# Keeping the last expert's block of the first layer on chip, and spreading the last combining products of the second

## The chip, the cores and the metric

The program runs on one core of one Trainium2 chip. The metric is the device time of one launch in microseconds (us): the median of three runs of the kernel before is 1739.39 us, with 1738.43 and 1743.01 us as the lowest and the highest. One more launch was recorded by the hardware profiler. All rows of a profile in this document come from that launch, and its times are counted from the start of its span.

The engines are named as the profile names them: PE (TensorE, matrix products; PEld is its weight load), DVE (VectorE), ACT (ScalarE), POOL (GpSimd) and SP (SyncE, which here only issues transfers). A name with a q, such as ACTq or SPq, is the engine's sequencer, which issues transfers and waits for semaphores.

## The reference

Two layers work on 512 tokens of `x` and 256 tokens of `ctx`, with 1024 features each, all in fp32.

```
for i in range(2):
    mod, modc = silu(c) @ mod_w[i] + mod_b[i], silu(c_ctx) @ mod_w[i] + mod_b[i]   # 6 parts each
    hx, hc = modulate(rmsnorm(x, ln1_g[i])), modulate(rmsnorm(ctx, ln1_g[i]))
    yx, yc = mixer_ab(hx, hc) if i == 0 else mixer_cd(hx, hc)
    x = x + g1 * yx
    hx = modulate(rmsnorm(x, ln2_g[i]))
    if i == 1:
        x = x + g2 * moe(hx)                       # 512 tokens
    else:
        ctx = ctx + g1c * yc
        out = moe(concat(modulate(rmsnorm(ctx)), hx))   # 768 tokens
        ctx = ctx + g2c * out[:256];  x = x + g2 * out[256:]
```

`moe` picks one of four groups and in it two of eight experts for each token. Each of the 32 experts computes `(silu(x @ w_gate) * (x @ w_up)) @ w_down` on its own tokens (1024 to 512 to 1024 features). The result, times the token's weight, is added to the token's row. `mixer_cd` of the second layer needs, for each token, the finished sum over its experts of the first layer: it starts with an RMS norm over the whole row, a modulation by a scale and a shift for each feature, and a product with `w_in_cd`, whose columns are the queries (512), the keys and values (256) and the pooled branch `u` (512).

## The kernel before

**Experts.** The experts are visited in an order of 32 steps, n = 0 to 31. Each step gathers up to 64 tokens (a second block of 64 is computed only where an expert has more than 64), and runs gate and up products (`mm_gate_up`, L1488, eight steps of k with one 512 KB page of weights each), `hidden`, `hidden_T` and the down products (`mm_down`, L1511, four pages). A block of 64 tokens fills 128 partitions: partitions 0 to 63 hold the first 512 features of the result and partitions 64 to 127 the last 512. The weights come through SP as pages of 512 KB in the order in which they are used.

**The end of a step in layer 0** (`main0`, L1556). `down(n)` multiplies the result by the token's weight and `g2` into a tile `ys` (`times_gate`, L1385: one ACT and two DVE instructions), and `scatter(n, 0)` adds its rows into the array `xD` in HBM with an indirect transfer of POOL (L1394). A second block has the same instructions for `ys`, and its store stands in a branch that POOL takes only for a count above 64. After step 31 come `next_weights(1, 2)`, which issues the first two pages of the query weights on ACT's queue, and `mixer_cd_in`.

**The start of the next mixer** (`mixer_cd_in`, L1813). Token tiles of 128 rows are handled in the order `seq = [0, 1, 4, 5, 2, 3]`; tiles 4 and 5 are `ctx` and have no queries and no `u`. `x_load` reads a tile X from `xD` on SP. `wkv`, `wq` and `wu` are weights that are split into a high and a low part: a step is one ACT instruction (`high`, L292) and one DVE instruction (`low`, L297) for each page, and frees the page. `rows(t)` makes the sum of squares on ACT (L271) and, when its second half `normed` is called, the factor (DVE L264, POOL L266) and the scaled rows `y` (DVE L1833). `trans(t)` transposes `y` on PE (L1848), applies scale and shift (six ACT instructions L1861 and two DVE instructions L1859) and splits the result into `hi` and `lo` (DVE L1863, L1864). In the loop over tiles, turn i projects tile i (`qkv`: 48 products, 24 for a `ctx` tile), then runs `rows` for tile i+2 and `trans` for tile i+1, the transposes of tile i-1's queries and keys, the 24 products `pu` of the branch `u`, and `qk_norm` and `qk_rotate`, whose last DVE instruction is L385. In turn 0 the four pages of `wu` are split between `qkv` and `rows`.

**Order and buffers.** In these stages every engine executes its instructions in the order in which the program writes them (`by_hand(4)` and `by_hand(5)`; only stages 3 and 6 leave some engines to the planner, L43). `sm` (L93) hands out four PSUM banks in turn, so a fifth small product waits until one of the last four has been read. `pages` (L99) hands out 4 KB pages of each partition, the longest free first; a transfer or an instruction that writes a page waits for the last reader of what it held before.

**Layer 1** (`main1`, L1598). The results of two steps are kept on chip as `hi` and `lo`, and are added to the token tiles by products with a one-hot matrix: `combine` (L1435) makes eight units, one for each half c of the features and each token tile t, of two products and one addition. For t = 1 of the very last pair the addition goes over ACT and POOL. During the gate and up products of the next odd step, `beside` (L1606) runs two units after each of k = 5, 6 and 7, and the rest after the last k. After step 31 the eight units of the last pair run at once, each followed by a store of 256 KB to the output on SP (L1620).

Of the kernel before, what the change touches and what calls it, by code (L numbers as in the profile page):

```python
# [7 lines left out]
F32 = mybir.dt.float32  # L8
# [62 lines left out]
def hybrid_dit_kernel(ctx: ExitStack, tc: tile.TileContext, a, out):  # L71
# [1250 lines left out]
    class Experts:  # L1322
# [112 lines left out]
        def combine(self, m, oh, then=None):  # L1435

            def unit(c, t):
                ps = sm("cmb")
                for i, y in enumerate(self.hl[m]):
                    nc.tensor.matmul(ps, oh[:, tok(t)], y[:, c * 512:(c + 1) * 512], start=(i == 0), stop=(i == 1))  # L1440
                if then and t % 3 == 1:
                    x, y = X(t)[:, c * 512:(c + 1) * 512], self.wp.tile([128, D], F32, tag="ys", name="ys", bufs=1)[:, 0:512]
                    nc.scalar.activation(y, ps, AF.Copy)
                    nc.gpsimd.tensor_tensor(x, x, y, OP.add)  # L1444
                else:
                    self.add(t, c, ps)
                if then:
                    then(t, c)

            return [lambda c=c, t=t: unit(c, t) for c in range(2) for t in range(self.nt)]  # L1450

        def block(self, b, w, tk):

# [102 lines left out]
        def main0(self):  # L1556
# [3 lines left out]
            NP = NE // 2  # L1560

            def down(n):
                t, e = hT[n], order[n]
                self.mm_down(self.yy[:, 0, :], 0, t, W[n, 2])
                when(cnti[0:1, e:e + 1], [PE], lambda: self.mm_down(self.yy[:, 1, :], 1, t, W[n, 2]))
                self.used((n, 2))
                self.scatter(n, 0)()
                when(cnti[0:1, e:e + 1], [POOL], self.scatter(n, 1))

# [28 lines left out]
        def main1(self):  # L1598
# [6 lines left out]

            def beside(n, k):  # L1606
                self.used_page((n, k // 4), k % 4)
                for _ in range(2 if k >= 5 else 0):
                    if units:
                        units.pop(0)()  # L1610

# [201 lines left out]
    def mixer_cd_in(m1, mk, work, QS, KS, v, us):  # L1813
# [11 lines left out]

        def rows(t):

            y = Y[t] = [pages.new("y", pools=[keep, m1] if t in seq[:2] else None) for _ in range(2)]
            ss = square_sum(mk, X(t), y[1])

# [61 lines left out]

        x_load(seq[0])
        run(wkv.steps)
        run(wq.steps)
        rest = load(a["w_in_cd"][1, 2:4], 2, [keep], nc.scalar)
        wq.raw.extend(rest)
        wq.step(rest[0])
# [3 lines left out]
            x_load(t)  # L1902
        wu = Split(load(a["w_in_cd"][2]), 512)
        router(1)
        rows(seq[0])()
        trans(seq[0])
        rows(seq[1])()
        for i, t in enumerate(seq):
            P[t] = big("qps")
# [149 lines left out]
        runs.append(run)  # L2059
        return run  # L2060

    runs, first = [], []

    def next_weights(i, n):
        first.append(load(a["w_in_cd"][i], n, [keep], nc.scalar))
# [147 lines left out]
```

## Time and profile before

| | |
|---|---|
| median of the runs | 1739.39 us (1738.43 to 1743.01) |
| the profiled launch's own time | 1740.23 us |
| its span, first to last instruction | 1738.6 us |
| PE busy | 1555.6 us, 89% of the span |
| DVE, ACT, POOL busy | 871.4, 498.0, 430.3 us |
| TensorE clock granted, mean | 0.965 of full speed |
| DMA, mean over the span | 306 GB/s read and written |

Busy time is summed over the launch; which engine or transfer a stage waits for has to be read from that stage. In the rows of a timeline, the columns are the start (us), the duration (us), the engine, the line of the kernel, the operation, the tile written and the tiles read, the shape and the number of instructions merged into the row; the brackets hold the time that the engine stood idle before it and what ended the wait. Where several instructions are merged, the duration is that of the whole group.

### The profile page before, as it was taken

To read this page: it belongs to the slowest core of one execution; us is meant where nothing else is said; L and a number is where in the kernel's file an instruction comes from. 1 tells how busy PE (TensorE), PEld (TensorE's weight loads), DVE (VectorE), ACT (ScalarE), POOL (GpSimd) and SP (SyncE) were. 2 spreads that over 40 slices of the span, in tenths; PEclk is the share of its full clock that TensorE was granted. 3 is DMA by queue.
4 is the path that set the end of the run, shared out by engine and by line. 5 is a ranking of instruction groups with operands and counts; after the bars stand their busy time and mean duration, and the time that the engine had idled before them with its cause. 6 is when DMAs were issued, how large, how long until landed. Compare 5 with 4: busy or idle time off the path is not lost. (4 is left out here: it accounts for less than half of the span.)

```text
span 1738.6 us, 23632 instructions
## 1 busy us (share of the span) xinstructions
PE 1555.6 (89%) x8524; PEld 823.2 (47%) x8524; DVE 871.4 (50%) x1674; ACT 498.0 (29%) x998; POOL 430.3 (25%) x376
## 2 busy tenths in 40 slices
PE   5979689998799999999987589989699999999996
PEld 4868457887333333333322477668433343232332
DVE  3797889788333332233232565775533443343334
ACT  3422458833111111111111443482211211111111
POOL 2535555132122122112111222310112212121110
PEclk9999889999799999999999899999799999999998
DMA  9211833356899999999999524623899999999996
GB/s 369 64 65 69 314 135 147 110 197 238 333 392 398 400 385 383 397 388 389 397 394 397 218 74 181 239 89 131 319 410 409 408 409 408 408 408 408 408 410 235
DMA packets 151567, 518.65 MB, mean 298 GB/s; under 512 B 22444, under 2 KB 23180, under 8 KB 151436
## 3 DMA queue, kind: packets, MB, share of 16 engines
q1 hardware_dynamic: 136748, 488.58, 71.8%
q0 software_dynamic: 11520, 16.81, 3.7%
q10 hardware_dynamic: 3168, 11.54, 1.7%
q8 instruction: 79, 1.29, 0.3%
q14 instruction: 52, 0.43, 0.1%
HBM read 510.49 MB, written 21.02 MB: 306 GB/s over the span
## 5 line engine op out<-in xcount | busy, mean ns | idle before, releaser
L1492 PE MATMUL gu<-w,xt 128*64 128x512 f32 x2304 | 535.4, 602 | 23.4 <-DMA w<-in_ex_dram 19.1
L1492 PEld LDWEIGHTS gu<-w,xt 128*64 128x64 f32 x2304 | 151.2, 137 | 348.1 <-issue 240.8
L1514 PE MATMUL yy<-w,ht 128*64 128x512 f32 x1152 | 272.5, 608 | 15.4 <-DMA w<-in_ex_dram 6.6
L1499 DVE TENSOR_TENSOR hh<-hh,gu 128x512 f32<-128x512 f32 (+1 forms) x64 | 35.4, 553 | 356.2 <-ACT hh L1498 356.2
L1498 ACT ACTIVATE hh<-gu 128x512 f32<-128x512 f32 (+1 forms) x64 | 31.4, 490 | 612.5 <-PE gu L1492 336.9
L1514 PEld LDWEIGHTS yy<-w,ht 128*64 128x64 f32 x1152 | 78.1, 138 | 183.5 <-issue 133.3
L1394 POOL DMA_INDIRECT xD<-ys,sidx x40 | 71.1, 1777 | 317.0 <-DVE ys L1390 314.5
L1405 DVE TENSOR_TENSOR X<-X,cmb 128x512 f32<-128x512 f32 x126 | 79.6, 683 | 99.9 <-PE cmb L1440 99.8
L1424 POOL TENSOR_TENSOR lo<-ys,hi 64x512 fp32r<-64x512 f32 x58 | 72.5, 1268 | 217.0 <-ACT hi L1423 217.0
L1367 POOL DMA_INDIRECT Xg<-hD,gidx x40 | 41.9, 1048 | 263.2 <-PE xtp L1476 243.6
L751 DVE SCALAR_TENSOR_TENSOR acc<-glu,convp,acc 128x784 f32<-128x784 f32 x76 | 97.9, 1288 | 1.6
L762 POOL TENSOR_TENSOR part<-part,prod 128x784 f32<-128x784 f32 x40 | 84.7, 2118 | 43.2 <-ACT prod L761 42.3
L1390 DVE TENSOR_TENSOR ys<-yy,ys 128x512 f32<-128x512 f32 x64 | 44.3, 692 | 96.9 <-PEq L1305 52.8
L266 POOL TENSOR_TENSOR rs<-ms,mhalf 128x1 f32<-128x1 f32 (+2 forms) x40 | 41.4, 1036 | 170.8 <-DVE ms L264 170.2
L1423 ACT ACTIVATE hi<-ys 64x512 fp32r<-64x512 f32 x64 | 40.2, 629 | 139.7 <-DVE ys L1401 139.7
L524 PE MATMUL ptp<-cst,P 128*128 128x128 f32 x368 | 52.9, 283 | 18.6 <-POOL P L512 10.5
L1508 DVE COPY ht<-htp 128x512 f32<-128x512 f32 (+1 forms) x64 | 35.4, 553 | 66.6 <-PE htp L1506 66.6
L697 PE MATMUL qps<-wh,hi 128*128 128x256 f32 (+1 forms) x176 | 61.0, 347 | 8.0 <-DVE hi L1863 2.4
L532 ACT ACTIVATE pT<-ptp 128x512 f32<-128x512 f32 (+1 forms) x96 | 53.3, 589 | 44.8 <-PE ptp L524 44.1
L512 POOL TENSOR_SCALAR P<-P,rd 128x768 f32<-128x768 f32 (+3 forms) x40 | 33.2, 829 | 130.9 <-DVE rd L510 41.9
L502 ACT ACTIVATE P<-S,nm 128x768 f32<-128x768 f32 (+3 forms) x80 | 59.9, 757 | 13.1 <-DVE nm L495 8.3
L495 DVE TENSOR_REDUCE nm<-S 128x1 f32<-128x768 f32 (+3 forms) x80 | 58.6, 763 | 8.2 <-PE S L488 5.9
(310 smaller groups left out, 2551.2 us busy)
## 6 DMA issues: line engine op xcount, KB each, us to landing
w<-in_ex_dram SPq DMA_DIRECT2D x768, 512.0 KB
w<-in_mod_w_dram SPq DMA_DIRECT2D x96, 512.0 KB
w<-in_w_out_dram SPq DMA_DIRECT2D x16, 512.0 KB
w<-in_w_in_ab_dram SPq DMA_DIRECT2D x14, 512.0 KB
hD<-x ACTq DMA_DIRECT2D x8, 512.0 KB
xD<-X ACTq DMA_DIRECT2D x6, 512.0 KB
w<-in_w_in_cd_dram ACTq DMA_DIRECT2D x6, 512.0 KB
X<-xD SPq DMA_DIRECT2D x6, 512.0 KB
```

The costliest lines, as they stand in the source:

```text
L495: nc.vector.tensor_reduce(nm, u["S"][h][:, u["span"]], AX.X, OP.max, negate=True)
L502: nc.scalar.activation(u["P"][h][:, :n], u["S"][h][:, u["span"]], AF.Exp, bias=nm, accum_out=u["den"][:, h:h + 1])
L524: nc.tensor.transpose(ps[:, (c - c0) * 128:(c - c0 + 1) * 128], u["P"][c // nk][:, c % nk * 128:(c % nk + 1) * 128], ident)
L532: nc.scalar.activation(dst, src, AF.Copy)
L697: nc.tensor.matmul(ps[:, o:o + n], h(x, k, tk), w(p, k, 0, n), start=(k == 0 and c == 0), stop=(k == KT - 1 and c == 2))
L751: nc.vector.scalar_tensor_tensor(acc, glu[:, ct, i:i + CW], w(i), acc, OP.mult, OP.add)
L762: nc.gpsimd.tensor_tensor(self.part[ct], self.part[ct], t, OP.add)
L1394: return nc.gpsimd.indirect_dma_start(out=xD[:, :], out_offset=bass.IndirectOffsetOnAxis(ap=idx, axis=0), in_=ys[:, :], in_offset=None, bo ...
L1405: nc.vector.tensor_tensor(x, x, ps, OP.add)
L1424: eng.tensor_tensor(lo[rows, c], ys[rows, c], hi[rows, c].bitcast(F32), OP.subtract)
L1492: nc.tensor.matmul(self.gu[c * 64:(c + 1) * 64, b, :], xt[:, k, q * 64:(q + 1) * 64], w[k][:, c * 512:(c + 1) * 512], start=(k == 0), stop ...
L1514: nc.tensor.matmul(yy[c * 64:(c + 1) * 64], t[:, b, f % 2, f // 2, :], w[f][:, c * 512:(c + 1) * 512], start=(f == 0), stop=(f == 3))
```

## The change

There are three edits.

1. In layer 0, the first block of expert step 31 is not scattered to HBM. Its rows `ys` are split into `hl` (a high part by an ACT copy and a low part by a DVE subtraction), and a one-hot matrix `oh` (768 columns, one for each token) is made from a POOL iota and a DVE comparison. Each `rows(t)` of the next mixer then multiplies `oh` and `hl` on PE (four products of 64 rows with 512 columns, two for each half of the features) and adds the two results to the loaded tile X on DVE, ahead of the sum of squares. The conditional store of a second block stays. `oh` and `hl` hold two pages until the last tile.
2. In `mixer_cd_in`, `rows` of the first tile comes between the splits of `wkv` and of the first two pages of `wq`; `normed` and `trans` of that tile come ahead of the load of the other two pages of `wq` (`rest`), of their splits, of the loads of the other five tiles and of the load of `wu`.
3. In layer 1, step 31 runs one combining unit after each k in place of two after each of the last three; and the eight units of a pair take the token tiles in the order 1, 0, 2, 3 in place of 0, 1, 2, 3.

```diff
@@ combine @@
-            return [lambda c=c, t=t: unit(c, t) for c in range(2) for t in range(self.nt)]
+            return [lambda c=c, t=t: unit(c, t) for c in range(2) for t in sorted(range(self.nt), key=lambda t: t % 3 != 1)]
@@ main0, down(n) @@
-                t, e = hT[n], order[n]
+                t, e, r = hT[n], order[n], self.route
+                if n == NE - 1:
+
+                    oh = pages.new("oh", F32R, (128, self.ntok), [keep])
+                    it, hl = pages.new("iotai", I32, (128, self.ntok)), pages.new("hl", F32R, (128, 2, 512), [keep])
+                    nc.gpsimd.iota(it, pattern=[[1, self.ntok]], base=0, channel_multiplier=0)
+                    nc.vector.tensor_scalar(oh, it, r.tok[:, 0, e:e + 1], None, op0=OP.is_equal)
+                    pages.done([it])
...
+                if n == NE - 1:
+                    ys = self.times_gate(0, r.ws[:, 0, e:e + 1], r.wc[:, 0, e:e + 1])
+                    nc.scalar.activation(hl[:, 0, :], ys, AF.Copy)
+                    nc.vector.tensor_tensor(hl[:, 1, :], ys, hl[:, 0, :].bitcast(F32), OP.subtract)
+                    when(cnti[0:1, e:e + 1], [POOL], self.scatter(n, 1))
+                    kept.extend((oh, hl))
+                    return
                 self.scatter(n, 0)()
@@ main1, beside(n, k) @@
-                for _ in range(2 if k >= 5 else 0):
+                for _ in range(1 if n == NE - 1 else 2 if k >= 5 else 0):
@@ mixer_cd_in, rows(t) @@
+            oh, hl = kept
+            for c in range(2):
+                part, ps = slice(c * 64, (c + 1) * 64), sm("cmb")
+                for i in range(2):
+                    nc.tensor.matmul(ps, oh[part, tok(t)], hl[part, i, :], start=(i == 0), stop=(i == 1))
+                x = X(t)[:, c * 512:(c + 1) * 512]
+                nc.vector.tensor_tensor(x, x, ps, OP.add)
+            if t == seq[-1]:
+                pages.done(kept)
@@ mixer_cd_in @@
         x_load(seq[0])
         run(wkv.steps)
+        normed = rows(seq[0])
         run(wq.steps)
+        normed()
+        trans(seq[0])
         rest = load(a["w_in_cd"][1, 2:4], 2, [keep], nc.scalar)
...
         wu = Split(load(a["w_in_cd"][2]), 512)
         router(1)
-        rows(seq[0])()
-        trans(seq[0])
         rows(seq[1])()
```

## Rows read from the trace of the kernel before

**Rows 1.** The windows view of four stretches from the end of layer 0's experts to the start of the next attention. The columns are the stretch, its length, the busy time and number of instructions of PE, PEld, DVE, ACT and POOL, the granted TensorE clock, the DMA share and GB/s.

```profile
968.00:982.00 14.00, 0.05 (x1) 0.08 (x2) 11.05 (x14) 4.67 (x6) 9.75 (x10) 0.68 0.69 227
...
996.10:1010.90 14.80, 14.80 (x82) 12.75 (x81) 8.95 (x16) 5.42 (x13) 4.03 (x3) 1.00 0.00 1
1010.90:1037.40 26.50, 20.35 (x135) 17.90 (x132) 17.60 (x37) 14.86 (x38) 6.83 (x8) 0.94 0.24 80
1037.40:1072.00 34.60, 34.60 (x190) 29.14 (x194) 18.51 (x35) 8.19 (x19) 9.21 (x8) 0.95 0.25 83
```

**Rows 2.** The timeline of PE over the same stretch: the first transposes of the mixer, the first projection, the first product `pu`, and the first product of the projections of tiles 1 and 2.

```profile
981.95 1.94 PE L1848 MATMUL tp<-cst,y 128*128 128x128 f32 x8 [14.14 <-DVE y L1833]
985.33 0.55 PE L697 MATMUL qps<-wh,hi 128*128 128x256 f32 x1 [1.44 <-ACT y L1861]
...
996.92 0.47 PE L697 MATMUL pu<-wh,hi 128*128 128x512 f32 x1
...
1002.48 0.39 PE L697 MATMUL qps<-wh,hi 128*128 128x512 f32 x1
...
1037.40 0.50 PE L697 MATMUL qps<-wh,hi 128*128 128x512 f32 x1 [2.41 <-DVE hi L1863]
```

**Rows 3.** The timelines of DVE, POOL, SP and ACT between layer 0's last down products and those transposes: the last expert's result, its scatter, the loads of the six tiles, the first sum of squares and the scaled rows.

```profile
967.95 0.69 DVE L1390 TENSOR_TENSOR ys<-yy,ys 128x512 f32<-128x512 f32 x1 [3.19 <-PEq L1305]
...
968.91 1.81 POOL L1394 DMA_INDIRECT xD<-ys,sidx  x1 [14.74 <-DVE ys L1390]
...
975.42 2.73 SPq L1824 DMA_DIRECT2D X<-xD  x6
...
979.03 1.06 ACT L271 ACTIVATE y<-X 128x1024 f32<-128x1024 f32 x1 [3.85 <-DMA X<-xD]
...
981.05 0.75 DVE L1833 TENSOR_SCALAR y<-X,rs 128x1024 f32<-128x1024 f32 x1 [0.69 <-POOL rs L266]
```

**Rows 4.** The timelines of ACT and DVE over the splitting of `wkv` and `wq`: two issues of `wq` pages, the two steps of `wkv`, the two issues of `rest` and the step on its second page, and DVE's six steps in one row.

```profile
963.13 0.86 ACTq L132 DMA_DIRECT2D w<-in_w_in_cd_dram  x2
964.17 2.00 ACT L292 ACTIVATE wh<-w 128x1024 fp32r<-128x1024 f32 x2 [0.55 <-DMA w<-in_ex_dram]
...
968.71 0.82 ACTq L132 DMA_DIRECT2D w<-in_w_in_cd_dram  x2
...
974.12 1.06 ACT L292 ACTIVATE wh<-w 128x1024 fp32r<-128x1024 f32 x1 [0.82 <-DMA w<-in_w_in_cd_dram]
...
970.42 7.76 DVE L297 TENSOR_TENSOR wl<-w,wh 128x1024 fp32r<-128x1024 f32 x6
```

**Rows 5.** The timelines of ACT, SP and DVE around the first transposes: the six modulations of tile 0, the issue of the four pages of `wu`, ACT's first and last step on them, DVE's four steps on them, and the first modulation on DVE of tile 1.

```profile
983.12 2.20 ACT L1861 ACTIVATE y<-tp,modT,A 128x128 f32<-128x128 f32 x6 [2.94 <-issue]
...
987.79 1.06 ACT L292 ACTIVATE wh<-w 128x1024 fp32r<-128x1024 f32 x1 [1.43 <-DMA w<-in_w_in_cd_dram]
...
991.63 1.06 ACT L292 ACTIVATE wh<-w 128x1024 fp32r<-128x1024 f32 x1 [0.16 <-DMA w<-in_w_in_cd_dram]
...
978.24 2.67 SPq L132 DMA_DIRECT2D w<-in_w_in_cd_dram  x4
...
988.88 5.18 DVE L297 TENSOR_TENSOR wl<-w,wh 128x1024 fp32r<-128x1024 f32 x4
...
998.02 0.41 DVE L1859 TENSOR_SCALAR y<-tp,A,modT 128x128 f32<-128x128 f32 x1 [2.49 <-ACT y L1861]
```

**Rows 6.** The timeline of DVE in turns 1 to 3 of the loop over tiles: three times the last instruction of a turn's `qk_rotate` and the next tile's first modulation.

```profile
1009.69 0.42 DVE L385 TENSOR_TENSOR ks<-qn,ks 128x256 fp32r<-128x256 f32 x1
...
1012.69 0.41 DVE L1859 TENSOR_SCALAR y<-tp,A,modT 128x128 f32<-128x128 f32 x1 [0.21 <-ACT y L1861]
...
1025.04 0.42 DVE L385 TENSOR_TENSOR ks<-qn,ks 128x256 fp32r<-128x256 f32 x1
...
1027.73 0.41 DVE L1859 TENSOR_SCALAR y<-tp,A,modT 128x128 f32<-128x128 f32 x1
...
1033.95 0.43 DVE L385 TENSOR_TENSOR ks<-qn,ks 128x256 fp32r<-128x256 f32 x1 [1.02 <-ACT ks L382]
...
1036.48 0.41 DVE L1859 TENSOR_SCALAR y<-tp,A,modT 128x128 f32<-128x128 f32 x1
```

**Rows 7.** Two groups of the lines view over the whole span: the addition of a PSUM bank to a tile, and the high part of `ys` in layer 1. The columns are the line, the engine, the operation, tiles and shapes, the count, the busy time in us and the mean of one in ns, the idle time before and what ended it.

```profile
L1405 DVE TENSOR_TENSOR X<-X,cmb 128x512 f32<-128x512 f32 x126 | 79.6, 683 | 99.9 <-PE cmb L1440 99.8
...
...
L1423 ACT ACTIVATE hi<-ys 64x512 fp32r<-64x512 f32 x64 | 40.2, 629 | 139.7 <-DVE ys L1401 139.7
```

**Rows 8.** The timelines of PE and DVE in the last step of layer 1: the gate and up products of k = 0 to 4, of k = 6 and of k = 7, the first product of the units between them and of those after k = 7, and DVE's last four additions.

```profile
1705.61 4.46 PE L1492 MATMUL gu<-w,xt 128*64 128x512 f32 x20
...
1712.39 1.08 PE L1492 MATMUL gu<-w,xt 128*64 128x512 f32 x4
1713.40 0.50 PE L1440 MATMUL cmb<-hi,oh 128*128 128x512 f32 x1
...
1714.53 1.08 PE L1492 MATMUL gu<-w,xt 128*64 128x512 f32 x4
...
1716.31 2.48 DVE L1405 TENSOR_TENSOR X<-X,cmb 128x512 f32<-128x512 f32 x4 [0.85 <-PE cmb L1440]
```

**Rows 9.** The timelines of POOL and SP at the end of the span: the first addition of POOL to a tile, and the eight stores of the output, of which the first starts at the time shown and the other seven follow that addition.

```profile
1729.86 1.29 POOL L1444 TENSOR_TENSOR X<-X,ys 128x512 f32<-128x512 f32 x1 [39.30 <-ACT ys L1443]
...
1729.61 5.35 SPq L1620 DMA_DIRECT2D out_dram<-X  x8
```

More of the change, by code (lines that the diff above doesn't have):

```diff
@@ L2060, in extra_slot @@
         return run
-    runs, first = [], []
+    runs, first, kept = [], [], []
     def next_weights(i, n):
```

## The prediction

> **What bounds the kernel now.** I read the busy shares first: PE is busy for most of the span, so a change is worth what it does to stretches in which PE waits. The windows view shows where these are. Between 968 and 982 us PE does next to nothing; up to 1010.9 and again from 1037.4 to 1072 us it is busy throughout; between 1010.9 and 1037.4 it idles 6.2 of 26.5 us [rows 1]. PE's timeline gives the waits: 14.14 us for the scaled rows of the first tile, and 2.41 us for DVE's `hi` of tile 2 at 1037.40 [rows 2]. The other engines' timelines say what lies in the 14.14 us. The last result is ready at 968.64, its scatter starts at 968.91, SP issues the tile loads at 975.42, ACT squares at 979.03, DVE writes `y` at 981.05 [rows 3]. The wait covers other work: ACT and DVE split `wkv` and `wq` in it, DVE until 978.2 [rows 4], and SP issues `wu` in it [rows 5]. In the loop over tiles the chain passes DVE, ACT and POOL in turn: from a turn's last L385 to the next tile's L1859 there are only 2.1 to 2.6 us [rows 6].
>
> The sum is made against the profiled launch, 1740.23 us; its span is 1738.6, so 1.63 us lie around it. The median is 0.84 us below it. All engines here keep program order, so I walk the new order with the old durations.
>
> **Edit 1 and 2, up to the first transposes.** The scatter of step 31 and the wait for it go. The tile load then waits for the scatter of step 30, long past, and is free. What is late next is the sum itself. `ys` ends at 967.95 + 0.69 = 968.64. ACT's copy takes 0.63, as L1423 does [rows 7]; the subtraction takes 0.69, as the multiplication of the same size did [rows 3]: `hl` is ready at 970.05. The scatter's second `ys`, scale and rope stand next in DVE's queue and took from 968.64 to 970.42 [rows 3, 4], 1.78: DVE is free at 971.85. ACT waited for `ys` too: behind its copy are queued the second block's copy, the issue of the first `wq` pages (at 963.13 before), and the splits of `wkv` (at 964.17 before) [rows 4], now at about 970 to 972. The two `low` steps of `wkv`, 7.76 / 6 = 1.29 each [rows 4], end at 974.5. The four products have run by then. I bound one, which has 64 rows where before shows none so shaped in this stage, by nothing and by 0.6, and both are covered by the `low` steps. Two additions, 2.48 / 4 = 0.62 each [rows 8], 0.68 by the group [rows 7], end at 975.8. The square holds ACT until 977.0. Then come the two `high` steps of `wq` (2.0), whose `low` steps end at 980.75, and only behind them, in DVE's queue, the factor and `y` (0.75). From the square's start to the start of `y` there were 2.02 us, of them 1.06 for the square itself [rows 3], so the factor, with POOL, takes 0.9: `y` ends at 982.4. PE starts at 982.5 in place of 981.95. The expected gain of several us is a loss of 0.5; I take 0.5 and keep 0 to 1; a gain is excluded as long as DVE keeps its order.
>
> **Edit 2, after the first transposes.** `rest` was issued at 968.71 and used at 974.12 for its second page [rows 4], inside the wait. Now its issue stands behind six instructions L1861, which ended at 985.32 [rows 5]: 985.8. Of the five other tile loads, the last takes the page of tile 0's `y` (walking the list of free pages), which the transposes free at about 984.5, and `wu`, issued at 978.24 before [rows 5], stands behind it on SP. So seven pages are asked for between 984.7 and 987.2. Pages land (991.63 - 987.79) / 3 = 1.28 us apart [rows 5], and the second page of `rest` took 5.41 us [rows 4], so 2.85 ahead of the first. Alone it would land at 991.2; as the last of the seven at 984.7 + 2.85 + 7 x 1.28 = 996.5. In order of issue it is the fifth: 994.0, which I take.
>
> From there one queue follows another. ACT splits that page until 995.1, DVE until 996.4. Only then come tile 1's additions (997.7), its square on ACT, and 2.05 after the square's start (979.03 to 981.05 [rows 3]) its `y`, until 1000.5. ACT's steps on `wu` stand behind that square, so that DVE's four steps, 5.18 [rows 5], run from 1000.5 to 1005.7; before, they ran from 988.88 beside the first projection. Behind them are the additions of the third tile (1007.0), its square, factor and `y` (1009.8), and behind these tile 1's first L1859: 1009.8 in place of 998.02 [rows 5], 11.8 late. PE can't fill this: the products of the third tile's rows and the transposes of tile 1 hold all four small banks, so `pu` waits for the first of those additions (1006.4 in place of 996.92 [rows 2]). With the landing at 991.2 the delay is 9.0, at 996.5 it is 14.3.
>
> **The loop.** From the end of L385 to the next L1859 there were 2.58, 2.27 and 2.10 us [rows 6], 6.95 in all, because the square could run during the projection. Now the products of `rows` stand behind the projection on PE and the additions behind L385 on DVE: 1.3 + 2.05 + 0.75 + 0.1 = 4.2 us a tile, 12.6 in all: 5.65 more. It ends with tile 2's projection (1037.40), after which no tile has `rows` left, and PE is busy without a gap to 1072 [rows 1], so nothing takes the delay back. The extra products on PE, at most 24 at some 0.3 us, lie in the waits. The iota and the comparison for `oh` lie beside the down products, where POOL waits 14.74 us and DVE 3.19 [rows 3]. Sum up to here: 11.8 + 5.65 = 17.45 us, which includes the 0.5; ends 14.65 and 19.95.
>
> **Edit 3.** In step 31 of layer 1, k = 0 to 4 take 4.46 us, 0.89 each [rows 8]; beside units a k takes 1.01 (1712.39 to 1713.40) and two units 1.13 (to 1714.53). Changing between the two kinds so costs about 0.12, a unit 0.5, and a step with one unit 1.63. Eight are 13.0: the last product ends at 1718.65 and its addition 0.75 later, 1719.4. Before, the additions ended at 1716.31 + 2.48 = 1718.8 [rows 8], and `hidden` waits for them on DVE. Without any change cost it would be 1717.5, with each unit at the price of two (2.14) 1723.5. I take +0.6, with ends of -1.3 and +4.7. The new order of tiles: POOL's first addition (1729.86) can start 0.47 earlier, but behind it SP then has eight stores to issue in place of seven, at 5.35 / 8 or less each [rows 9]. I take 0, within 0.4 either way.
>
> **Sum.** 17.45 + 0.6 = 18.05: 1758.3 on the profiled launch, 1757.4 on the median. Its own range is 1753 to 1761.
>
> **Rivals.**
> *The shorter round trip wins (not slower).* If `rows` were not held behind the splits, the chain from `hl` at 970.05 would be products 1.9, additions 1.3, square to `y` 2.05, `y` 0.75: 976.1, 5.9 us ahead of 981.95. With the later transfers hidden and edit 3 it gives 1739.39 - 5.9 + 0.6 = 1734.1. For it speaks PE's empty window [rows 1]; against it that DVE's steps on `wu` and `y` come in program order in the trace [rows 5]. It decides if the additions come within about 5 us of `hl`. Chance 0.07. The Trainium skill, page "PSUM — Partial Sum Buffer", section "Engine vs sequencer instructions", says that the queues of ScalarE, VectorE and GpSimd are strictly first in, first out. By that rule this rival falls, and the trace agrees as far as it goes: DVE's six steps from 970.42 to 978.18 run unbroken in program order.
> *The late weights are absorbed.* If `rest` and `wu` came in time behind the first projection, only the 0.5, the 5.65 of the loop and 0.6 remain: 1746.1. For it: the first 24 products need only `wkv`. Against it: `rest` would have to land some 10 us earlier than reckoned. Chance 0.12.
> *PE falls behind too.* `pu` would start after about 5 us without products. In the empty window the clock was granted at 0.68 on the mean [rows 1]; at the lower level of 1.2 GHz 24 products of about 0.23 cost up to 5.5 us more, some 3.5 of them beyond DVE's slack: 1761 to 1764. Chance 0.16.
> *The tile load still waits for the branch of the second block on POOL.* Then it is issued at about 971.6 and lands 3.6 later, 0.7 after DVE wants it: 1758. Chance 0.03.
>
> **Numbers.** The forecast itself has 0.62. Two launches of this kernel are told apart from about 0.3% on, 5.2 us: 1734.2 to 1744.6 counts as the same. Half of the first rival is faster, 0.04; its other half, the edge of the second and what I may have missed give 0.09 for the same; 0.87 for slower. The range 1746 to 1764 leaves out the first rival and the ends of the others.
>
> **What would show it.** After: PE's wait ahead of the first transposes still near 14 us, ended by `y`; `rest` issued on ACT after L1861, and ACT and DVE waiting for it; DVE's four steps on `wu` after 1000 us; a PE wait of about 5 us ahead of `pu`, ended by an addition of DVE; 4.2 us between L385 and L1859; DVE's last addition of step 31 later against the down products. The forecast is wrong if `y` of the first tile comes before 978 us, or if the steps on `wu` end by 997 us.

## The result, and the profile after

The changed kernel takes 1760.49 us (median of 4 runs, 1759.25 to 1762.0) against 1740.06 us before on the same chip (4 runs, 1738.43 to 1743.01): 1.011 times as long, 95% interval 1.0095 to 1.0126, which is 16.5 to 21.9 us. The forecast was 1757.4. The profiled launch has a span of 1758.4 us and a mean granted clock of 0.960.

In this profile layer 0 ends 2.30 us earlier than in the one of before: the last `yy` (L1514) starts at 961.85 instead of 964.15. All comparisons of places are therefore made from that start. In the after-kernel the modulation of `trans` is L1884 on ACT and L1882 on DVE (L1861 and L1859 before), `y` is L1856, the additions are L1848, the products with `oh` are L1846.

PE's timeline of the changed kernel, to be read beside [rows 2]:

```profile
980.12 1.97 PE L1871 MATMUL tp<-cst,y 128*128 128x128 f32 x8 [11.61 <-DVE y L1856]
...
1001.99 0.76 PE L697 MATMUL pu<-wh,hi 128*128 128x512 f32 x1 [4.68 <-DVE X L1848]
...
1051.93 0.55 PE L697 MATMUL qps<-wh,hi 128*128 128x512 f32 x1 [3.44 <-DVE hi L1886]
```

The wait ahead of the first transposes has not gone: they start 18.27 us behind the last `yy`, where it was 17.80. `pu` and tile 2's projection now begin late as well, behind DVE. DVE's timeline shows with what (each row of L1848 is both halves of a tile):

```profile
972.72 1.27 DVE L1848 TENSOR_TENSOR X<-X,cmb 128x512 f32<-128x512 f32 x2
976.20 2.36 DVE L297 TENSOR_TENSOR wl<-w,wh 128x1024 fp32r<-128x1024 f32 x2 [2.21 <-ACT wh L292]
...
979.31 0.75 DVE L1856 TENSOR_SCALAR y<-X,rs 128x1024 f32<-128x1024 f32 x1 [0.69 <-POOL rs L266]
...
992.09 1.28 DVE L1848 TENSOR_TENSOR X<-X,cmb 128x512 f32<-128x512 f32 x2
...
996.07 5.17 DVE L297 TENSOR_TENSOR wl<-w,wh 128x1024 fp32r<-128x1024 f32 x4
1001.16 1.28 DVE L1848 TENSOR_TENSOR X<-X,cmb 128x512 f32<-128x512 f32 x2
...
1005.14 0.40 DVE L1882 TENSOR_SCALAR y<-tp,A,modT 128x128 f32<-128x128 f32 x1
...
1016.80 0.42 DVE L385 TENSOR_TENSOR ks<-qn,ks 128x256 fp32r<-128x256 f32 x1
1019.56 1.28 DVE L1848 TENSOR_TENSOR X<-X,cmb 128x512 f32<-128x512 f32 x2 [2.34 <-PE cmb L1846]
...
1023.54 0.41 DVE L1882 TENSOR_SCALAR y<-tp,A,modT 128x128 f32<-128x128 f32 x1
...
1035.88 0.41 DVE L385 TENSOR_TENSOR ks<-qn,ks 128x256 fp32r<-128x256 f32 x1
...
1040.19 0.41 DVE L1882 TENSOR_SCALAR y<-tp,A,modT 128x128 f32<-128x128 f32 x1
...
1046.41 0.42 DVE L385 TENSOR_TENSOR ks<-qn,ks 128x256 fp32r<-128x256 f32 x1 [1.02 <-ACT ks L382]
...
1051.01 0.40 DVE L1882 TENSOR_SCALAR y<-tp,A,modT 128x128 f32<-128x128 f32 x1
```

The first additions end at 974.0, but `y` stands at 979.31, behind the steps of `wq`. The three gaps from L385 to the next L1882 are 6.74, 4.31 and 4.60 us from start to start (less L385's own 0.42 as the prediction counts them: 6.32, 3.90, 4.18), where [rows 6] have 2.58, 2.27 and 2.10. ACT's timeline has the two issues of `rest` and what then waits for them:

```profile
982.13 0.35 ACTq L132 DMA_DIRECT2D w<-in_w_in_cd_dram  x1
...
982.51 0.45 ACTq L132 DMA_DIRECT2D w<-in_w_in_cd_dram  x1
...
986.92 1.06 ACT L292 ACTIVATE wh<-w 128x1024 fp32r<-128x1024 f32 x1 [3.39 <-DMA w<-in_w_in_cd_dram]
989.85 1.06 ACT L292 ACTIVATE wh<-w 128x1024 fp32r<-128x1024 f32 x1 [1.88 <-DMA w<-in_w_in_cd_dram]
993.40 1.06 ACT L271 ACTIVATE y<-X 128x1024 f32<-128x1024 f32 x1 [2.49 <-DVE X L1848]
```

In the windows view (columns as in [rows 1]) PE idles 4.7 us between 997 and 1010.9, with a granted clock of 0.63 on the mean of that stretch, and 5.8 us in the stretch that [rows 1] show full. While the first products of `pu` run, behind the wait of 4.68 us, the clock is granted at 0.50, which is 1.2 GHz:

```profile
997.00:1010.90 13.90, 9.22 (x30) 7.19 (x29) 9.85 (x16) 5.34 (x12) 2.19 (x2) 0.63 0.00 1
1002.00:1007.60 5.60, 5.60 (x13) 4.42 (x14) 3.58 (x9) 4.00 (x10) 0.55 (x1) 0.50 0.00 0
1037.40:1072.00 34.60, 28.78 (x153) 23.95 (x152) 18.01 (x41) 12.43 (x33) 5.67 (x8) 0.90 0.32 109
```

### The profile page after: what moved, and what is told of

It is laid out like the page before. It is cut to its first block, busy times and chain, and to the rows that moved or that the text cites. A ratio compares the mean times of both kernels' runs of the same rounds, so it can differ in the third digit from the quotient of the medians.

```text
span 1758.4 us, 23706 instructions
## 1 busy us (share of the span) xinstructions
PE 1569.4 (89%) x8548; PEld 829.0 (47%) x8548; DVE 879.4 (50%) x1688; ACT 498.1 (28%) x999; POOL 426.2 (24%) x376
## 5 line engine op out<-in xcount | busy, mean ns | idle before, releaser
L1514 PE MATMUL yy<-w,ht 128*64 128x512 f32 x1152 | 269.4, 602 | 16.0 <-DMA w<-in_ex_dram 7.1
L1514 PEld LDWEIGHTS yy<-w,ht 128*64 128x64 f32 x1152 | 77.2, 137 | 181.9 <-issue 130.3
L1476 PE MATMUL xtp<-cst,Xg 128*128 128x128 f32 x384 | 50.5, 283 | 14.3 <-DMA Xg<-hD,gidx 9.4
```

The costliest lines, as they stand in the source:

```text
L1476: nc.tensor.transpose(ps[:, k * 128:(k + 1) * 128], src[:, (h * 4 + k) * 128:(h * 4 + k + 1) * 128], ident)
L1514: nc.tensor.matmul(yy[c * 64:(c + 1) * 64], t[:, b, f % 2, f // 2, :], w[f][:, c * 512:(c + 1) * 512], start=(f == 0), stop=(f == 3))
```

## The experiments

The table holds what PE's timeline gives for every run, in us behind the start of layer 0's last `yy`: the first, second and third tile's transposes, and the first product of attention's scores (L484). The last column but two is the time from there to the first gate/up product of layer 1. Medians and ratios to before are those of the timed runs; each ratio is to runs of before taken beside that run, whose medians lie between 1740.06 and 1742.2 us, so it isn't the quotient of two medians of the table. In edit3_only and in bank_pool_lows the last `yy` itself waits 1.12 and 2.38 us for its weights, which is inside their figures.

| kernel | tile 0 | tile 1 | third | scores | to layer 1 | median | ratio (95%) |
|---|---|---|---|---|---|---|---|
| before | 17.80 | 31.98 | 46.71 | 106.03 | 179.68 | 1740.06 | 1 |
| before_again | 17.77 | 32.43 | 47.16 | 106.56 | 182.19 | 1743.39 | one run |
| edit3_only | 18.70 | 32.39 | 47.12 | 104.98 | 184.38 | 1740.83 | 0.9997 (0.9983 to 1.001) |
| before_pool_lows | 17.13 | 31.42 | 46.15 | 105.58 | 181.86 | 1742.59 | 1.0003 (0.9989 to 1.0017) |
| after | 18.27 | 34.36 | 57.61 | 122.77 | 183.43 | 1760.49 | 1.011 (1.0095 to 1.0126) |
| chip_only | 18.56 | 34.67 | 57.85 | 122.95 | 183.49 | 1760.78 | 1.0102 (1.0082 to 1.0122) |
| early_loads | 18.86 | 33.43 | 52.87 | 118.95 | 184.88 | 1757.56 | 1.0084 (1.0062 to 1.0106) |
| late_one_tile | 18.26 | 32.08 | 47.93 | 109.71 | 179.96 | 1747.77 | 1.003 (1.0016 to 1.0045) |
| early_one_tile | 18.24 | 32.12 | 46.95 | 104.91 | 184.06 | 1744.57 | 1.001 (0.9995 to 1.0025) |
| sums_first | 18.25 | 34.25 | 55.21 | 122.29 | 184.57 | 1762.97 | 1.0124 (1.0102 to 1.0145) |
| sums_in_wait | 18.89 | 33.35 | 55.66 | 115.40 | 188.49 | 1759.78 | 1.0114 (1.0098 to 1.0129) |
| all_early | 12.31 | 26.05 | 50.55 | 109.00 | 184.67 | 1747.80 | 1.0039 (1.0025 to 1.0052) |
| all_early_bank | 12.16 | 25.91 | 43.18 | 105.56 | 180.80 | 1743.15 | 1.001 (0.9996 to 1.0023) |
| bank_pool_lows | 14.95 | 31.83 | 49.61 | 112.55 | 185.14 | 1749.18 | 1.0043 (1.0028 to 1.0057) |

**The edits apart.** chip_only takes edit 3 out of the changed kernel, edit3_only puts it alone into the one before.

```diff
# chip_only, against after
-            return [lambda c=c, t=t: unit(c, t) for c in range(2) for t in sorted(range(self.nt), key=lambda t: t % 3 != 1)]
+            return [lambda c=c, t=t: unit(c, t) for c in range(2) for t in range(self.nt)]
...
-                for _ in range(1 if n == NE - 1 else 2 if k >= 5 else 0):
+                for _ in range(2 if k >= 5 else 0):
```

> The changed kernel without edit 3 (edits 1 and 2 alone). Theory: edit 3 costs 0.95 us ahead of the last down products and about 1.5 us at the output stores, so this lands 2.4 us below the changed kernel, near 1758 us (ratio to before 1.0103), with 13.6 us again from the first gate and up product of the last step to its hidden transposes and the first output store 1.6 us ahead of the second. Rival (the new order of the units is free at the stores, as my forecast had it): about 1 us below the changed kernel, near 1759.5. Rival (edit 3 is worth something and the first two edits cost more): above 1760.5.

> The kernel before with edit 3 alone. Theory: 14.5 us in place of 13.6 from the last step's first gate and up product to its hidden transposes, and an output whose eight stores all start behind POOL's first addition, so that the first of them no longer goes ahead: 2.4 us slower than before, near 1742.5. Rival (nothing at the stores): 1741. Rival (a gain, since waits for weights are filled): 1739 or less.

Without edit 3 the changed kernel is not faster (1760.78), so the expected 2.4 us are not there, and edit 3 alone is level with before, as the rival without a cost at the stores had it. Edit 3 costs nothing that these runs can tell, at most 0.1% by the interval of edit3_only: the loss is edits 1 and 2.

**Late loads or additions.** Edits 1 and 2 do two things: they put loads and splits later, and they add products, additions and squares that wait for them. Three runs make a square of the two.

```diff
# early_loads, against after (compute in the same order; the old places of these loads are left out)
+        rest = load(a["w_in_cd"][1, 2:4], 2, [keep], nc.scalar)
+        for t in seq:
+            x_load(t)
+        wu = Split(load(a["w_in_cd"][2], pools=[work]), 512)
-        x_load(seq[0])
         run(wkv.steps)
...
# early_one_tile and late_one_tile: this in rows(t) of early_loads and of after
-            for c in range(2):
+            for c in range(2 if t == seq[0] else 0):
```

> The changed kernel with the issues of the rest of the query weights, of all six tile loads and of the branch weights put ahead of everything in the mixer; the order of all computing instructions is as in the changed kernel. Theory (the order in the queues of DVE and ACT is the greater part): the four DVE steps on the branch weights end 3.7 us earlier than in the changed kernel, PE is no longer behind in turn 1 (2.3 us), in all 6 us less: near 1754.5. Rival (the late landing alone is the cost): 11 us less or more, 1749 or below. Rival (landing is not what gates): no change, 1760.

> The same early issues, and the products with the one-hot matrix and their additions for the first tile only: the last expert's first block is left out of the other five tiles. Theory: the remaining delay of the branch weights and the loop is made by these additions, so from L385 to the next modulation it is 2.1 to 2.6 us again, and with edit 3's 2.4 us the kernel comes to 1743. Rival (it is the new place of the first tile's rows ahead of the splits that costs, not the additions): within 2 us of the run with early issues, 1753 or more.

> The changed kernel, late loads and third edit included, but the last block is left out of five of the six tiles: only the first tile has products and additions. With early_loads and early_one_tile it makes a square of four (loads late or early, additions for six tiles or one). Theory (lateness and additions add up, the additions being four fifths): early loads were worth 3.2 us with all additions and are worth about as much here, 1744.6 + 3.2 = 1747.8 us. Rival (the late second half of wq and wu only cost because the additions and squares stand behind them): 1745, as with early loads. Rival (the late loads are the cause, and the additions only cost behind them): 1756 or more.

With all additions, early loads are worth 1760.49 - 1757.56 = 2.9 us; with one tile's 1747.77 - 1744.57 = 3.2. The additions of the other five tiles, with their products and what waits for them, cost 1760.49 - 1747.77 = 12.7 with late loads and 13.0 with early ones. The two add up, and what is left over before is 0.1% by early_one_tile's ratio and not told from nothing. So the additions are four fifths of what these four kernels differ by, and the loads one fifth. The intervals of a pair with late and early loads overlap, so the smaller share rests on the two pairs together and on the traces: at the scores the loads are 3.82 and 4.80 us, the additions 13.06 and 14.04. early_loads came out between its theory and the rival of no change; the other two came within 2 us of their theories.

The same split holds on the way to the second tile. Its first L1882 stands 9.42 us later than before in after (by the last `yy`), 5.79 later in early_loads, where ACT and DVE no longer wait for `rest` or `wu`, 4.39 in late_one_tile and 0.14 in early_one_tile:

```profile
1002.57 0.40 DVE L1882 TENSOR_SCALAR y<-tp,A,modT 128x128 f32<-128x128 f32 x1
```

This row is early_loads, on DVE's timeline, with its last `yy` at 962.91.

**The place in DVE's queue.** If 13 us are lost to where the additions stand, they should come back when these stand in a wait.

```diff
# sums_in_wait, against early_loads (rows split into prods, sums and norm)
-                rows(seq[i + 2])()
+                (norm if i else rows)(seq[i + 2])()
...
+            if i + 3 < TT:
+                prods(seq[i + 3])
             if t < XT:
                 pu = sm("pu")
-            Q[t] = qk_norm(1, t, P[t], t < XT, v, mk)
+            Q[t] = qk_norm(1, t, P[t], t < XT, v, mk, None, (lambda n: sums(seq[i + 3])) if i + 3 < TT else (lambda n: None))
```

> early_loads, in which the additions of the last three tiles are moved one turn ahead, into the wait of VectorE for GpSimd's power inside the query and key norm (2.08 us on an image tile, 0.81 on a context tile); their products stand ahead of pu on TensorE. The work is the same. Theory (the place in VectorE's queue costs, 4.2 us a tile: two additions, then the squares that can only start behind them): three turns give back 3 x 4.2 and pay 0.46 + 0.46 + 1.73 for additions longer than the wait, so 1757.6 - 10.0 = 1747.6 us. Rival (VectorE is short of time in this loop, so that the additions cost wherever they stand): only the wait for the squares goes, 3 x 1.2, 1754 us. Rival (the low clock of TensorE is what makes the turns long): nothing changes, 1757.

The expectation failed as a time. The trace says that two things happened. In the turns that it was meant for, the scores come 3.55 us earlier than in early_loads. From the third transposes to the scores it is 59.74 us where early_loads has 66.08 and before 59.32 (the granted clock over that stretch is 0.94, 0.90 and 0.94): the same work in another place gives back 6.34 of the 6.76 us that it cost there, more than the 3.6 that the first rival left, less than the 10.0 of the theory. How much of it is the clock that rose with it is not separated. But `pu` of the first turn starts later, at 40.15 instead of 36.46 behind the last `yy`, though nothing of DVE's that feeds it moved:

```profile
1002.74 0.80 PE L697 MATMUL pu<-wh,hi 128*128 128x512 f32 x1 [1.94 <-DVE y L1895]
```

It waits for DVE's modulation of the tile before (L1895 in this kernel): two more `cmb` tiles in the ring of four small PSUM banks give `pu` not the bank of the third tile's additions but one that DVE empties only with this modulation, behind those additions, their square and `y`. And the 3.55 us that reached the scores did not reach the end: from there to layer 1 this profile took 188.49 us, the most of all. The median of four runs, 1759.78, shows no gain either, so it is hardly one execution alone; what takes it back stays open.

**Everything early.** all_early is the version that the prediction's first rival asked for: additions of the first tile straight behind the products, every load first, no edit 3.

```diff
# all_early, against chip_only: main0, then the start of mixer_cd_in
                 hh = self.hidden(0, 2)
+                if n == NE - 1:
+                    next_weights(1, 4)
...
+        for t in seq:
+            x_load(t)
+        wu = Split(load(a["w_in_cd"][2], pools=[work]), 512)
...
+        prods(seq[0])
+        for w in wkv.raw:
+            wkv.high(w)
+        sums(seq[0])
+        wkv.low(wkv.raw[0])
+        normed = norm(seq[0])
+        highs(wq, slice(0, 3))
+        normed()
+        wkv.low(wkv.raw[1])
+        wq.low(wq.raw[0])
+        trans(seq[0])
...
# all_early_bank, against all_early
-            if i + 3 < TT:
+            if 0 < i and i + 3 < TT:
                 prods(seq[i + 3])
             if t < XT:
                 pu = sm("pu")
                 proj(pu, h(t), None, wu, 0, 512)
+            if i == 0:
+                prods(seq[3])
```

> The change without its third edit, with everything put where nothing waits for it: all loads first (the second projection's four pages already behind the last gate and up products), the first tile's products and additions ahead of the splits, scale columns and rope tables, the additions of tiles 2 and 3 behind the first transposes, those of the last three in the waits of the query and key norm. Theory (what the change takes off, the last block's way over memory, is worth up to 5 us once nothing stands in its place): first transposes at 13 to 14 us behind the last yy instead of 17.8 before, 2.7 us paid in the loop, so 1741.7 - 2 = 1739.5 us, between 1737 and 1741. Rival (the first projection then waits for its split weights, so the earlier transposes are worth nothing): 1744. Rival (the additions cost wherever they stand): 1752.

> all_early with one step moved: in the first turn the products of the fourth tile stand behind pu on TensorE, not ahead of it, so that pu's PSUM bank is one that VectorE has emptied before. Theory (the order in which the four small banks go round, not the work, made pu wait 6.2 us and then run at 1.2 GHz): the turn from the second to the third transposes falls from 24.5 us to about 15, so 1747.8 - 9 = 1739 us, level with before or a little under it. Rival (the additions themselves make the loop long): 1745 or more.

all_early failed its expectation, 1747.80 us instead of 1739.5. The first transposes come 5.5 us earlier than before, and a turn later all is lost: PE's timeline has the same wait for a bank as above, longer, and the products behind it take 0.63 us each instead of 0.39, at a granted clock of 0.51 in the windows view.

```profile
998.97 0.79 PE L697 MATMUL pu<-wh,hi 128*128 128x512 f32 x1 [6.16 <-DVE y L1892]
```

```profile
999.50:1004.20 4.70, 4.70 (x13) 3.62 (x12) 4.17 (x8) 0.00 (x0) 1.57 (x1) 0.51 0.02 3
```

One step moved, so that `pu` gets a bank emptied before, and PE's timeline of all_early_bank has no wait there:

```profile
975.63 1.97 PE L1881 MATMUL tp<-cst,y 128*128 128x128 f32 x8 [5.23 <-DVE y L1866]
...
990.23 0.48 PE L697 MATMUL pu<-wh,hi 128*128 128x512 f32 x1
```

The turn falls from 24.5 to 17.27 us and the median from 1747.80 to 1743.15, level with before and between its theory and its rival: the order of the banks was worth 4.7 us. It still wins nothing. Its first transposes lead by 5.64 us; at the second tile's first modulation on DVE 0.35 are left (33.52 behind the last `yy`, 33.87 before, from 998.02 in [rows 5]):

```profile
996.99 0.40 DVE L1892 TENSOR_SCALAR y<-tp,A,modT 128x128 f32<-128x128 f32 x1
```

Between the two stand, on DVE, steps of `wq` that used to lie in the wait for the tile, the additions of two tiles and a wait for the square of one of them. The old wait of 14.14 us held work that has to be done in any order.

That is DVE's side. On PE the third transposes still lead by 3.53 us (43.18 against 46.71), and the turn behind them takes it: the fourth stand at 62.44 instead of 59.02. There PE's timeline and windows view have

```profile
1011.82 0.66 PE L406 MATMUL ktp<-cst,ks 128*128 128x128 f32 x4 [1.93 <-DVE y L1892]
1012.48 2.13 PE L1845 MATMUL cmb<-hl,oh 64*128 64x512 f32 x4
1014.54 0.79 PE L697 MATMUL pu<-wh,hi 128*128 128x512 f32 x1
```

```profile
1014.50:1019.70 5.20, 5.20 (x13) 4.10 (x13) 4.28 (x9) 0.00 (x0) 2.56 (x2) 0.50 0.00 2
```

PE waits for DVE, and behind the wait four products of `cmb` take 2.13 us and the first of `pu` run at a granted clock of 0.50, 1.2 GHz, so that `pu` takes 8.2 us instead of 5.8. No run separates DVE's queue from the clock there.

**The bank in the changed kernel itself.**

```diff
# sums_first, against after
+                first_sums = rows(seq[2])
                 highs(wu, slice(0, 4))
                 for w in wu.raw:
                     wu.low(w)
+                first_sums()
-            if i + 2 < TT:
+            elif i + 2 < TT:
                 rows(seq[i + 2])()
```

> The changed kernel with one step moved: the additions of the third tile stand ahead of the four steps that split the low halves of wu on VectorE, not behind them. Theory (pu's first product waits for one of the four small PSUM banks, the one that these additions empty): pu starts some 2 us earlier (40.1 to about 38 us behind the last yy), then runs at the pace of the low halves, which come 2.5 us later, and ends about 4 us earlier: 1760.5 - 4 = 1756.5 us. Rival (pu waits for its split weights): it starts 2.5 us later, 1763. Rival (TensorE makes up for it later in the loop): 1760.

Both were half right. `pu` starts 2.6 us earlier (37.57 against 40.14), so it was the bank that held it; and it then waits for `wu`, whose high halves now stand behind a square on ACT:

```profile
1000.42 0.80 PE L697 MATMUL pu<-wh,hi 128*128 128x512 f32 x1 [2.22 <-ACT wh L292]
```

The scores come 0.5 us earlier and the time is no better. In the changed kernel `pu`'s wait for the bank alone is thus worth next to nothing. That DVE's queue is what comes last there is argued from its gaps above; this run doesn't show it.

**DVE's queue relieved.**

```diff
# bank_pool_lows, against all_early_bank; the second part alone in before_pool_lows
-        for w in wq.raw[1:]:
-            wq.low(w)
+        for j, w in enumerate(wq.raw[1:]):
+            wq.low(w, nc.gpsimd if j == 2 else nc.vector)
...
-                for w in wu.raw:
-                    wu.low(w)
+                for j, w in enumerate(wu.raw):
+                    wu.low(w, nc.gpsimd if j > 1 else nc.vector)
```

> all_early_bank with three of VectorE's subtractions (the low halves of one page of wq and two of wu, some 3.8 us of its queue) on GpSimd, which is idle there. Theory (the 5.6 us by which the first transposes come earlier are eaten by VectorE's queue up to the second tile's first L1892, 33.5 us behind the last yy against 33.9 before, because the splits that lay in the old wait now stand behind it): that step comes up to 3.8 us earlier, as far as TensorE (pu and the projections, 14.7 us a turn) lets it: 1743.2 - 2.5 = 1740.5 us, between 1739 and 1742, at or a little under before. Rival (TensorE alone sets the loop, so VectorE's queue is worth nothing): 1743. Rival (GpSimd's longer subtractions hold up pu): 1746.

> The kernel before with the low halves of two pages of wu (2.6 us of VectorE's queue) on GpSimd. It tells whether what bank_pool_lows may win comes from the change or from the moved subtractions alone. Theory (before, TensorE goes from the first projection over the second transposes to pu without a wait, so VectorE's queue has slack there): nothing, 1741.5 us, within 1.5. Rival (VectorE's queue sets the loop before as well): up to 2.6 less, 1739.

bank_pool_lows lost, and of its expectations the last rival came nearest. 2.4 us of it are waits for the last expert's weights ahead of the stage, in this profile; the rest stands in the timelines of DVE and POOL:

```profile
981.89 2.78 DVE L1897 TENSOR_TENSOR lo<-y,hi 128x512 fp32r<-128x512 f32 x1
```

```profile
981.52 2.60 POOL L297 TENSOR_TENSOR wl<-w,wh 128x1024 fp32r<-128x1024 f32 x1 [5.28 <-DMA rw<-in_rt_w_dram]
...
995.97 4.88 POOL L297 TENSOR_TENSOR wl<-w,wh 128x1024 fp32r<-128x1024 f32 x2 [4.57 <-DVE ms L264]
```

A subtraction of DVE that takes 0.69 us elsewhere took 2.78 while POOL subtracted, so little was taken off DVE, and POOL began the pages of `wu` only at 995.97 and held up the factor of the next tile, which stands behind them in its queue. Whether DVE's queue is the limit of all_early_bank was thus not tested cleanly. Before, the same two pages moved are worth nothing, as expected.

**The same kernel twice.**

> The kernel before, unchanged, for a second profile: how far the same instructions stand apart in two executions, stage by stage. Theory (the difference of 3.2 us in the first stretch of attention between before and after is the clock of that execution, not the change): this profile has the attention longer than the first one's, by 2 to 5 us, like edit3_only, and its layer 0 shorter or its total longer by as much. Rival (the change makes the attention longer): the same times as in the first profile, within 0.5 us.

From the scores to layer 1 it took 182.19 us, 2.5 more than the first profile of the same instructions; edit3_only, with the same instructions up to there, took 184.38. The windows view shows where most of it lies: between the first product of the scores and the first product `o` (L539), 13.67 us in the first profile of before (first row) and 17.53 in edit3_only (second row):

```profile
1070.20:1084.00 13.80, 11.08 (x91) 7.12 (x90) 10.76 (x31) 8.46 (x21) 3.15 (x4) 1.00 0.97 375
```

```profile
1066.00:1083.50 17.50, 15.24 (x89) 9.50 (x86) 10.77 (x31) 8.29 (x21) 3.16 (x4) 0.71 0.97 382
```

DVE and ACT are busy for nearly the same time; PE takes 4.2 us more, at a granted clock of 0.71 instead of 1.00. before_again has 15.30 us there at 0.89. after has 16.90 at 0.80, which is 3.23 of the 3.75 us by which it is longer than the first profile of before. The 3.75 us lie within what one kernel shows.

## Why the prediction was right, step by step

**The first transposes, +0.5.** Measured +0.47, by the mechanism named: `y` behind the steps of `wq`. But the same code stands between 17.13 and 18.70 in four profiles (1.12 of the 18.70 are a wait for weights), so the figure is confirmed in kind (no gain of 5.9 us) rather than to the tenth. The first rival, the shorter round trip, was refuted for this order of instructions, and all_early_bank shows more: even where the trip is really shortened, by 5.64 us, 0.35 of it is left at the second tile's modulation on DVE and 0.47 at the scores.

**The landing of `rest`, 994.0.** ACT began on the second page at 989.85, in before's time 992.15: 1.85 early, nearer the end "alone" (991.2) than I chose. Tile 1's first L1882 came 9.42 us late by the last `yy`, not 11.8, and the steps on `wu` began at 996.07, in before's time 998.37 instead of 1000.5. The step that failed is the place of `rest` in the queue of seven pages: I put its issue behind all six modulations, at 985.8, and ACT issued it among them, at 982.13 and 982.51, in before's time 984.43 and 984.81. SP issued `wu` from 982.49 on, so `rest` was ahead of most of those pages:

```profile
981.33 1.15 ACT L1884 ACTIVATE y<-tp,modT,A 128x128 f32<-128x128 f32 x3 [4.22 <-PE tp L1871]
...
982.71 0.82 ACT L1884 ACTIVATE y<-tp,modT,A 128x128 f32<-128x128 f32 x2
```

```profile
982.49 2.14 SPq L132 DMA_DIRECT2D w<-in_w_in_cd_dram  x4
```

**`pu` waits about 5 us for an addition of DVE.** 4.68 us, and by sums_first it was the PSUM bank. But there 2.57 us less of it were worth 0.48 at the scores: it was hardly on the path.

**The loop, +5.65.** The last two gaps, 3.90 and 4.18, are the 4.2 of the sum. The first is 6.32, because DVE waited 2.34 us for the products of `rows`: the mechanism of the rival "PE falls behind too", priced there at some 3.5 beyond DVE's slack. The first 13 products of `pu` follow each other at 0.43 us instead of 0.23 at the granted clock of 0.50, which puts the products of `rows`, behind them, 2.6 us later. The sum of the three is 14.40, so +7.45: here the term was too small.

**Sum up to tile 2's projection, +17.45.** At tile 2's L1882 it is 1051.01 - 961.85 = 89.16 against [rows 6]' 1036.48 - 964.15 = 72.33: +16.83. Two misses of 2.4 and 1.8 in opposite directions nearly cancel, which is luck. The three profiles with that code unchanged and the two with it changed agree at the scores: 105.86 and 122.86 on their means, +17.0. Nothing took it back in between, as said.

**Edit 3, +0.6.** A step of k with one unit takes 1.67 us in the trace (1.63 reckoned), and from the first gate/up product to the transposes of step 31 it is 14.51 instead of 13.56. But from the transposes of step 30 to those of step 31, 20.95 before, it is 20.52, since the step also begins earlier, and the runs show no difference. The step counted the stretch from a start that the edit's surroundings moved.

**Total, +18.05.** The measured difference of medians is 20.4, and 18.05 lies in its interval. Between the two profiles the spans differ by 19.8, and the pieces are these: layer 0 is 2.30 shorter, from the last `yy` to the scores it is 16.74 longer, from there to layer 1 3.75, and the rest 1.60. Only the second piece and the edit of layer 1 were forecast; most of the 3.75 is the clock of an execution, and that the total came out so near is in part luck. About 1.2 us of what is over lie where I forecast nothing: between the last transfer and the end of the span. In after it is

```profile
1755.50:1758.40 2.90, 0.00 (x0) 0.00 (x0) 0.00 (x0) 0.00 (x0) 0.00 (x0) 0.50 0.00 0
```

with nothing at work on any engine. Read in steps of 0.25 us, it is 1.75 in all four profiles without the kept block, 3.00 in after, and 2.75 to 4.25 in all ten with it. No row says what it is, and it stays open.

**The late weights absorbed (1746.1).** early_loads is this rival's condition, the loads in time and all additions, and it takes 1757.56: the price was wrong. It follows that the sum's split was wrong too. The sum has 11.8 us up to tile 1's L1859, of which this rival lets all but 0.5 go when the loads come in time; the loads are worth 3.6 to 4.3 of the measured 9.42, and 5.0 to 5.7 go with the additions of the second and third tile, which stand in the same chain on DVE with the squares and factors that wait for them. late_one_tile, the opposite case, takes 1747.77, and that this is near 1746.1 means nothing.

## What to carry to other kernels

A wait that ends with a transfer isn't free time if other engines fill it with work that the next stage needs: before pricing a shorter round trip, put that work where it would go and see what ends last then. An instruction added to an in-order queue costs its own time (1.28 us a tile here) and, here more than that, the chain that could run ahead and now can't (the squares and the factor behind it; 4.2 us a gap). And a buffer ring is an order too: two more tiles in a ring of four made a third, untouched user wait 6.16 us for a bank.

## What had not been expected

VectorE's 128x512 subtraction, 0.69 us alone, took 2.78 us when it met a 2.60 us subtraction on GpSimd: it ended 0.5 us behind GpSimd's, as if it had begun only then. The Trainium skill's page "SBUF — State Buffer", section "SBUF: two separate sides", says that the two engines share a pair of ports by an exclusive lock, held for a whole instruction, and that a VectorE instruction with two inputs in SBUF takes part in it against a GpSimd one that reads SBUF; this subtraction has two such inputs, and this trace agrees. The 4.7 us between all_early and all_early_bank, for one group of four products moved in PE's order, were more than any single instruction of the change costs. And the stretch from the scores to layer 1 differs by 4.7 us between executions of the same instructions (179.68 to 184.38), most of it before the first product `o` (13.67 to 17.53 us, at granted clocks of 1.00 to 0.71), while the three spans lie within 3.2 us (1738.6, 1739.4 and 1741.8): a difference of one stage between two single profiles needs a second profile before it is explained.
